# A hybrid attention layer on one core: loading the first gate's weight sums first, moving GLA's column products behind FoX's queries and keys, and making two of FF1's weight sums in DRAM

## The chip, the cores and the metric

The kernel runs on one core of a Trainium2 chip. The metric is the device time of one launch in microseconds (us); the median of three runs is given. A profile is taken of one further execution.

## What is computed

One layer of a streaming encoder for 512 frames of 1024 channels, all in float32. Three branches run side by side from the normalised input, are merged by gates, and a squared-ReLU MLP follows:

```python
u = rmsnorm(h, g_mix)
proj = u @ w_in          # GLA q,k,v,out-gate,alpha | FoX q,k,v,forget | memory q | 3 gates
o_gla = rmsnorm(gla_chunk_causal(gq * 64**-0.5, gk, gv, log_a), g_gla_head) * silu(gg)
o_fox = forgetting_attention(fq, fk, fv, log_sigmoid(ff + b_forget))   # 8 heads, causal
o_mem = memory_attention(mq, *split(rmsnorm(mem, g_mem) @ w_mem_kv))   # 256 tokens
gt = sigmoid(gates)
merged = gt[0] * (o_gla @ w_gla_o) + gt[1] * (o_fox @ w_fox_o) + gt[2] * (o_mem @ w_mem_o)
h = h + merged @ w_out
h = h + square(relu(rmsnorm(h, g_ffn) @ w_ff1)) @ w_ff2
return rmsnorm(h, g_final)
```

## The kernel before

Every product is made of three matmuls on halves that are split into a high part (a cast, on ScalarE, ACT) and a low part (the difference, on VectorE, DVE): high by high, high by low, low by high (`mm3`, L180 to L183). A weight tile is 128 x 1024; it is loaded by a DMA that SyncE (SP) issues (`load_w`, L164), cast (L171) and subtracted (L172), with three buffers of each kind in turn.

The larger products (GLA's values and output gate in `linear`, the three gates, FF1 and FF2) are Strassen-Winograd products: seven block products instead of eight, some of them of sums of weight blocks (named T for FF1 and the gates, G for `linear`) and of sums of u (named x or `xsum`, made by `u_sum` and split by `split`, L235). The sums of weights are made by DMAs that GpSimd (POOL) issues and that add to their destination (`accum_op`), in one of two ways:

- In DRAM, by `next_sum` (L134 to L146): behind each weight cast from the eighth on, POOL gets one DMA of a list, a copy (L143) or a sum (L141), that waits for that cast. The list before is `all_ops`: linear's G sums, then the T sums of FF1's first quarter. The later loads of G and T read these.
- In SBUF: a tile is loaded by SP and one or more sums are added to it. So it goes for the gates (`load_sum` L1207 and `plus` L1210, then the cast `high` L1223 and the low part `low` L1227), for FF1's quarters 1 to 3 (`sum_ring`, L1563 to L1578, with `tq`) and for FF2's factors (L1860).

The stages by time are: the front to 45 us; FoX's projections and softmax with products of other branches between them to 170; memory attention and the last of `linear` to 238; GLA to 298; the gates to 411; the merged output product to 480; FF1 and FF2 in four quarters to 817.

PE's order is written by hand, and a scheduler orders the others, but for sections under `in_order`, where ACT, DVE, SP (and in the gates POOL) keep the order of the code. The gates are such a section: the rounds begin with the raw loads that the first rounds want (`go(loads, 0)`), then the four T loads of the first gate, T1 and T2 for two halves each, then the sums into T1.

FoX's stage is a weave (L873): a list of steps on PE (scores, turns of the probabilities by matmuls with a unit matrix, L792 on, values) that draws units of other products between them, each with a share. Its filling list has, in order, FoX's pair 2 of queries and keys, the first sum of u, `linear(1)`, its split, pair 3, `linear(5)`, the second sum of u, `gla_k(0)`, `linear(2)`, the second split, `gla_q(0)` and `linear(6)`. `gla_k(0)` and `gla_q(0)` are column products of GLA's keys and queries. A softmax on DVE is custom operations on the scores (L781), reciprocals (L784) and a scaling of the probabilities `Pt` (L785), which the turns read. `u_sum` has three instructions for the first sum and two for the second, issued together behind a turn.

GLA begins with `decays(j)` (L1021): its matmuls read `la` (L1023), ACT makes `ex`, POOL sets one column of it (L1034), and DVE makes `kn` and three more of it, which PE turns (L1049).

Of the kernel before, what the change touches and what calls it, by code (L numbers as in the profile page):

```python
# [9 lines left out]
F32 = mybir.dt.float32  # L10
# [4 lines left out]
ALU = mybir.AluOpType  # L15
AX = mybir.AxisListType

P = 128
# [40 lines left out]
def hybrid_block(ctx, tc, chunks, wst, memT, xT, xN, gffn, gfin, wup, cst, out):  # L59
# [42 lines left out]

    tsum = {(n, i): dram.tile([1, P, 1024], F32, name=f"T{n}_{i}") for i in range(2) for n in (1, 2, 3, 4)}

    gsum = {n: dram.tile([2, P, 1024], F32, name=f"G{n}") for n in (1, 2, 3, 4)}

    def linear_ops():
        for n, src, add in ((1, "11", 0), (3, "12", 0), (1, "12", 1), (2, 1, 0), (2, "22", 1), (3, "22", 1), (4, 2, 0), (4, "21", 1)):  # L110
            if isinstance(src, str):
                i = index["N", "w_in", 4 * (src[0] == "2"), OFF["gv" if src[1] == "2" else "gg"]]
                src = wst[i:i + 2]
            else:
                src = gsum[src]
            yield gsum[n], src, add

    def sum_ops():
        for n, src, add in ((1, "11", 0), (3, "12", 0), (1, "12", 1), (3, "22", 1), (2, 1, 0), (2, "22", 1), (4, 2, 0), (4, "21", 1)):
            for i in range(2):  # L120
                k = index["F", 0, i, src] if isinstance(src, str) else None
                yield tsum[n, i], tsum[src, i] if k is None else wst[k:k + 1], add

    def all_ops():
        ff, lin = sum_ops(), linear_ops()
        for own in (3, 1, 1, 1, 1, 1):
            yield from islice(lin, own)
            yield from islice(ff, 1)
        yield from ff

    sums = all_ops()
    chunk_n, cast_now, low_now, hold = [0], [None], [None], [None]

    def next_sum(after):  # L134

        chunk_n[0] += 1
        if chunk_n[0] <= 7:
            return
        for to, src, add_ in islice(sums, 1):
            if add_:  # L140
                d = nc.gpsimd.dma_start(to, src, accum_op=ALU.add, max_dma_last_dim=8192)  # L141
            else:
                d = nc.gpsimd.dma_start(to, src)  # L143
            tc.add_manual_dep(d.ins, after.name, mybir.DependencyInfo(mybir.DependencyClass.Sync, mybir.DependencyReason.DATA),
                              reason="pace")

# [71 lines left out]
    def weave(steps, units, *gens, shares=None):  # L218

        fill = chain(*gens)  # L220
        done = 0
        shares = shares or [1] * len(steps)
        for i, st in enumerate(steps):
            st()
            due = units * sum(shares[:i + 1]) // sum(shares)
            while done < due and next(fill, fill) is not fill:
                done += 1
        run(fill)
# [306 lines left out]
    A11r, A12r, A21r, A22r = ([t[:, 4 * k:4 * k + 4, 256 * i:256 * i + 256] for t in (uhi, ulo)] for i in range(2) for k in range(2))  # L535
    A11, A12, A21, A22 = ([f(t) for t in a] for a in (A11r, A12r, A21r, A22r))

    def u_sum(n):

        x = xsum[n]  # L540
        if n == 1:
            nc.vector.tensor_tensor(x, A21[0], A22[0], op=ALU.subtract)
            nc.vector.tensor_tensor(x, x, A21[1], op=ALU.add)
            nc.vector.tensor_tensor(x, x, A22[1], op=ALU.subtract)
        else:
            nc.vector.tensor_tensor(x, xsum[1], A11[0], op=ALU.subtract)
            nc.vector.tensor_tensor(x, x, A11[1], op=ALU.subtract)

    def once(fn, *args):

        fn(*args)
        yield from ()
# [60 lines left out]
    with pool("fox") as xp:  # L613
# [211 lines left out]
        def gla_q(j):  # L825
            return proj(OFF["gq"] + P * j, lambda ps: nc.scalar.mul(gqT[j], ps, 0.125))

        def gla_k(j):
            return proj(OFF["gk"] + P * j, lambda ps: nc.scalar.copy(gkT[j], ps))
# [36 lines left out]
            early[n] = factor_tiles()  # L866
            split(*early[n], xsum[n])

        def early_sum(n):
            with tc.issue_after(live["turn"]):  # L870
                u_sum(n)

        weave([partial(fn, i) for fn, i, _ in steps], 80, fox_pair(2), once(early_sum, 1), linear(1, A11r), once(early_split, 1), fox_pair(3),  # L873
              linear(5, lambda: early[1]), once(early_sum, 2), gla_k(0), linear(2, A12r), once(early_split, 2), gla_q(0),
              linear(6, lambda: early[2]), shares=[n for *_, n in steps])


    mp = mst.enter_context(pool("merge", side="right"))
# [288 lines left out]
    with pool("outp") as op_:  # L1167
# [17 lines left out]
        def vec(to, x, y, op=ALU.add):  # L1185
            return nc.vector.tensor_tensor(to, x, y, op=op).ins
# [115 lines left out]
        def merge(g, i, c, half):  # L1302
            t = 2 * i + half
            x, a = th[g, i, c][:, half], half_of(acc[t], c)
            if g == 0:
                nc.vector.scalar_tensor_tensor(a, x, 1.0, a, op0=ALU.add, op1=ALU.mult)
            else:
                nc.vector.scalar_tensor_tensor(x, x, 1.0, half_of(ymem[t], c), op0=ALU.add, op1=ALU.mult)
                vec(a, a, x)

        def last_merge(c, t):
            x, a = th[2, t // 2, c][:, t % 2], half_of(acc[t], c)
# [53 lines left out]
        def go(when, i):  # L1366
            for fn, args in when.get(i, []):
                fn(*args)
# [3 lines left out]
        mh = ml = None  # L1372
        hN, now = [], [rounds[0]]
        with in_order(mybir.EngineType.Pool):
            go(loads, 0)
            loads[0] = []
            for other in range(2):
                for n in range(2):
                    load_sum(0, n, other)
            for n in range(2):  # L1380
                plus(0, n, 0, "12")
            for i, r in enumerate(rounds):
                now[0] = r
                if r == (2, 7):
                    omst.close()
                    mhp = late.enter_context(pool("mhl"))
                    mh, ml = (mhp.tile([P, KT, S], F32R, name=x) for x in ("mh", "ml"))
                if r == ("Y", 0):
                    hN += [h_tile(t, "h") for t in range(NT)]
                    gf = hp.tile([P, D], F32, tag="gf", name="gf")  # L1390
                    for t in (2, 3, 0, 1):
                        nc.sync.dma_start(hN[t], xN[t * P:(t + 1) * P, :])
                    nc.sync.dma_start(gf, gffn)
                if r == ("O", 0):
                    mst.close()
                    unp.append(late.enter_context(pool("un")))
                go(loads, i)
                go(early, i)
                n = NT if r[0] in ("Y", "O") else 2
                parts, due = todo[:1], [(r2, c) for r2 in rounds[i + 1:i + 2] for c in range(2)]  # L1400
                del todo[:1]
                for x in parts:
                    merge(*x)
                if i:
                    evac(rounds[i - 1], NT - 1 if rounds[i - 1][0] in ("Y", "O") else 1)
                for t in range(n):
                    mms(r, t)
                    if t == 0:
                        for x in due:
                            high(*x)  # L1410
                            low(*x)
                        bend()
                        go(after, i)
                    else:
                        evac(r, t - 1)
                    if r == ("Y", 0):
                        turn(t, 1)
                    if r == ("O", 1):
                        turn(t, 0)
            evac(r, n - 1)  # L1420
# [76 lines left out]
    with pool("ff") as yp:  # L1497
# [55 lines left out]
        def block(q, n, i):  # L1553
            if i > 1:
                return wst[index["B", q, i - 2, "21"]]
            if n in (1, 2, 3):
                return wst[index["F", q, i, {1: "11", 2: "21", 3: "22"}[n]]]
            n = {5: 1, 6: 2, 7: 3, 4: 4}[n]
            return tsum[n, i][0]

        tq = [yp.tile([P, 1024], F32, name=f"tq{i}") for i in range(2)]

        def sum_ring(q, n, i):  # L1563

            def plus(to, b):
                nc.gpsimd.dma_start(to, wst[index["F", q, i, b]], accum_op=ALU.add)

            if n == 7:
                raw = fetch(wst[index["F", q, i, "12"]])
                plus(raw, "22")  # L1570
                return split_b(raw)
            if n == 5:
                nc.sync.dma_start(tq[i], wst[index["F", q, i, "11"]])
                plus(tq[i], "12")
            w = split_b(tq[i])
            if n != 4:
                plus(tq[i], {5: "22", 6: "21"}[n])
            return w  # L1578

        def first_quarter():  # L1580
# [234 lines left out]

        def first_product(q, n):
            for i in range(2):
                w = sum_ring(q, n, i) if n in (5, 6, 7, 4) else ring(block(q, n, i))
                if n in (1, 5):
                    joint_product(n, w, (ev if n == 1 else od)[i][:, 1, :])  # L1820
                    continue
                ps = mmt([P, 2, 256])
                run(first_mms(n, w, ps))
                first_evac(n, i, ps)
# [365 lines left out]
```

## Time and profile before

| | |
|---|---|
| median of three runs | 820.36 us (819.77 to 821.3) |
| the profiled execution | 819.1 us |
| its span | 817.3 us |
| mean granted clock of PE | 0.988 |
| PE busy | 794.9 us, 97% |
| DVE busy | 621.5 us, 76% |
| ACT busy | 475.7 us, 58% |
| POOL busy | 100.1 us, 12% |
| PE's longest single wait | 5.7 us, for ACT's hi (L1223) |
| moved from DRAM | 156.25 MB, 214 GB/s over the span |

PE's share of the span is 97%. Its matmuls are pipelined, so a busy time can hold matmuls at half speed: the granted clock in a window tells. The view of waits lists how long PE stood, for which engine and line. The DMA share is the mean busy share of the 16 DMA engines of the core.

### The profile page before, as it was taken

The numbers are of one execution on the slowest core, as the hardware profiler recorded it, in microseconds if no ns is written. First come the engines' busy times: TensorE is split into PE (matmuls) and PEld (weight loads), VectorE is DVE, ScalarE is ACT, GpSimd is POOL, SyncE is SP. The second block draws the span as 40 slices with busy tenths as digits, with TensorE's granted clock in tenths as the row PEclk, the third lists the DMA queues.
The fourth block names the chain that finished last, engine by engine and source line by source line (L and its number), as shares of the span: only waits on it lengthen the run. The fifth ranks groups of instructions, "written<-read, shape, count | busy, mean of one in ns | idle before, by whom it ended". The sixth has DMA issues, their size and how long they took to land.

```text
span 817.3 us, 11675 instructions
## 1 busy us (share of the span) xinstructions
PE 794.9 (97%) x4351; PEld 677.8 (83%) x4351; DVE 621.5 (76%) x971; ACT 475.7 (58%) x746; POOL 100.1 (12%) x137
## 2 busy tenths in 40 slices
PE   9999989999999987999999999999999999999995
PEld 7888868888888875888888889977997899889974
DVE  6878989755876757667776558788789778987896
ACT  7756666634564345556434446864676367646854
POOL 0001001110200212020200001012110211111011
PEclk9999999999999997999999999999999999999998
DMA  9355768892832259988926318998999998998653
GB/s 355 135 164 165 234 237 217 264 267 78 254 108 83 73 178 189 250 191 248 204 80 242 121 50 237 296 229 214 224 247 215 220 235 231 216 251 226 156 90 116
DMA packets 42249, 159.15 MB, mean 195 GB/s; under 512 B 4944, under 2 KB 5648, under 8 KB 40976
## 3 DMA queue, kind: packets, MB, share of 16 engines
q0 software_dynamic: 13120, 58.73, 36.3%
q1 hardware_dynamic: 27712, 95.72, 32.2%
q10 hardware_dynamic: 1360, 3.96, 1.5%
q8 instruction: 34, 0.56, 0.3%
q14 instruction: 23, 0.19, 0.1%
HBM read 156.25 MB, written 18.91 MB: 214 GB/s over the span
## 4 chain that ended last, share of the span: by engine, by line
PE 78%; DVE 8%; DMA 8%; issue 3%; ACT 2%; POOL 0%; SPq 0%; POOLq 0%; DVEq 0%; ACTq 0%
PE mm L181 15%; PE mm L182 15%; PE mm L183 14%; PE mm L1462 10%; DMA b<-in_wst_dram 4%; PE a L182 4%; PE a L183 4%; PE a L181 4%; PE mm L1810 3%; DMA wb<-in_wst_dram 2%; PE mm L412 1%; PE mm L1811 1%; PE a L425 1%; DVE wlo L172 1%; DVE lo L1598 1%
## 5 line engine op out<-in xcount | busy, mean ns | idle before, releaser
L172 DVE TENSOR_TENSOR wlo<-raw,whi 128x1024 fp32r<-128x1024 f32 x44 | 53.8, 1224 | 30.6 <-ACT whi L171 29.8
L171 ACT CAST whi<-raw 128x1024 fp32r<-128x1024 f32 x44 | 46.3, 1053 | 49.2 <-PE mm L182 14.9
L1462 PE MATMUL mm<-u,hi 128*128 128x256 f32 x384 | 64.7, 283 | 0.0
L1462 PEld LDWEIGHTS mm<-u,hi 128*128 128x128 f32 x384 | 56.4, 189 | 0.1
L182 PE MATMUL mm<-lo,ch 128*128 128x512 f32 (+1 forms) x132 | 51.4, 389 | 0.9 <-DVE lo L1522 0.9
L183 PE MATMUL mm<-hi,cl 128*128 128x512 f32 (+1 forms) x132 | 51.0, 386 | 0.0
L181 PE MATMUL mm<-hi,ch 128*128 128x512 f32 (+1 forms) x132 | 51.0, 386 | 0.0
L1521 ACT CAST hi<-raw 128x1024 fp32r<-128x1024 f32 x34 | 35.8, 1053 | 25.8 <-PE mm L1462 12.2
L1522 DVE TENSOR_TENSOR lo<-raw,hi 128x1024 fp32r<-128x1024 f32 x34 | 41.6, 1223 | 10.3 <-ACT hi L1521 10.3
L1462 PE MATMUL mm<-u,lo 128*128 128x256 f32 x192 | 47.5, 283 | 0.0
L1462 PE MATMUL mm<-u2s,hi 128*128 128x256 f32 x288 | 47.3, 283 | 0.0
L1521 ACT CAST hi<-b 128x1024 fp32r<-128x1024 f32 x26 | 27.3, 1050 | 31.5 <-PE mm L183 19.4
L181 PE MATMUL mm<-uhl,whi 128*128 128x512 f32 x112 | 44.6, 398 | 0.0
L1860 POOL DMA_DIRECT2D b<-in_wst_dram x30 | 25.9, 874 | 146.3 <-DMA b<-in_wst_dram 43.8
L1227 DVE TENSOR_TENSOR lo<-wb,hi 128x1024 fp32r<-128x1024 f32 x21 | 25.3, 1223 | 24.2 <-ACT hi L1223 24.2
L183 PE MATMUL mm<-uhl,wlo 128*128 128x512 f32 x112 | 43.7, 390 | 0.0
L182 PE MATMUL mm<-uhl,whi 128*128 128x512 f32 x112 | 43.7, 390 | 0.0
L1462 PEld LDWEIGHTS mm<-u2s,hi 128*128 128x128 f32 x288 | 41.6, 190 | 0.0
L1522 DVE TENSOR_TENSOR lo<-b,hi 128x1024 fp32r<-128x1024 f32 x26 | 31.5, 1223 | 9.2 <-ACT hi L1521 9.2
L182 PE MATMUL a<-lo,ch 128*128 128x512 f32 (+1 forms) x96 | 37.3, 389 | 1.1 <-DVE lo L1598 0.7
L181 PE MATMUL a<-hi,ch 128*128 128x512 f32 (+1 forms) x96 | 37.2, 387 | 0.4 <-DVE h L1515 0.4
L183 PE MATMUL a<-hi,cl 128*128 128x512 f32 (+1 forms) x96 | 37.0, 386 | 0.0
(535 smaller groups left out, 2398.4 us busy)
## 6 DMA issues: line engine op xcount, KB each, us to landing
raw<-in_wst_dram SPq DMA_DIRECT2D x114, 512.0 KB
b<-in_wst_dram POOLq DMA_DIRECT2D x32, 512.0 KB, 6.7
wb<-in_wst_dram POOLq DMA_DIRECT2D x24, 512.0 KB, 7.9
tq<-in_wst_dram POOLq DMA_DIRECT2D x18, 512.0 KB, 9.6
b<-in_wst_dram SPq DMA_DIRECT2D x16, 512.0 KB
T<-in_wst_dram POOLq DMA_DIRECT2D x12, 512.0 KB, 5.8
wb<-in_wst_dram SPq DMA_DIRECT2D x12, 512.0 KB
G<-in_wst_dram POOLq DMA_DIRECT2D x4, 1024.0 KB, 9.1
```

The source lines that it names most:

```text
L171: cast = nc.scalar.copy(hi, raw)
L172: low_now[0] = nc.vector.tensor_tensor(lo, raw, f(hi), op=ALU.subtract).ins
L181: nc.tensor.matmul(ps, lh, rh, start=start, stop=False, skip_group_check=on)
L182: nc.tensor.matmul(ps, lh, rl, start=False, stop=False, skip_group_check=on)
L183: nc.tensor.matmul(ps, ll, rh, start=False, stop=stop, skip_group_check=on)
L412: nc.tensor.matmul(kps[h], w[:, h * P:(h + 1) * P], x[:, k, :], start=k == p == 0, stop=k == KT - 1 and p == 2)
L1227: nc.vector.tensor_tensor(lo, source(r, c), f(hi), op=ALU.subtract)
L1462: nc.tensor.matmul(ps[:, a, :], x[:, a, k, :], y[:, s, k, :], start=start, stop=stop, skip_group_check=go is not None)
L1521: split_now[0] = nc.scalar.copy(hi, raw).ins
L1522: split_now[1] = nc.vector.tensor_tensor(lo, raw, f(hi), op=ALU.subtract).ins
L1810: nc.tensor.matmul(ps, wh[:, a, k, :], u[:, k], start=k == 0, stop=False, skip_group_check=True)
L1860: nc.gpsimd.dma_start(to[i], wst[index["B", q, i, x]], accum_op=ALU.add)
```

## The change

It has three parts.

**First gate.** The loads of T1 and the sums into it stand before the raw loads, and T2's loads behind them. On SP, in the place where the gates begin (`wb` are the T tiles, `raw` weights as they are), before:

```order
L164 DMA raw_2964<-in_wst_dram 128x1024
L164 DMA raw_2998<-in_wst_dram 128x1024
L164 DMA raw_3026<-in_wst_dram 128x1024
L164 DMA raw_3028<-in_wst_dram 128x1024
L164 DMA raw_3030<-in_wst_dram 128x1024
L1207 DMA wb_3022<-in_wst_dram 128x1024
L1207 DMA wb_3023<-in_wst_dram 128x1024
L1207 DMA wb_3024<-in_wst_dram 128x1024
L1207 DMA wb_3025<-in_wst_dram 128x1024
```

and on SP at the same place after the change:

```order
L169 DMA raw_2976<-in_wst_dram 128x1024
L169 DMA raw_3010<-in_wst_dram 128x1024
L1208 DMA wb_3034<-in_wst_dram 128x1024
L1208 DMA wb_3035<-in_wst_dram 128x1024
L169 DMA raw_3042<-in_wst_dram 128x1024
L169 DMA raw_3044<-in_wst_dram 128x1024
L169 DMA raw_3046<-in_wst_dram 128x1024
L1208 DMA wb_3036<-in_wst_dram 128x1024
L1208 DMA wb_3037<-in_wst_dram 128x1024
```

T1's two loads moved ahead of three raw loads, and T2's two stay behind them.

**FoX's weave.** `gla_k(0)` comes right behind FoX's pair 2, where `linear(1)` was begun, and the rest follows it in the order of the diff; the sums of u are issued one instruction at a time. On DVE, the end of the second of the four softmaxes (`ri` reciprocals, `Pt` probabilities, `s` the split of the first sum of u, `oT` the values of the step before, `wlo` a weight's low part), before:

```order
L785 TENSOR_SCALAR Pt_1091<-Pt_1091,ri_1057 128x128
L235 TENSOR_TENSOR s_1277<-x_470,s_1276 128x1024
L785 TENSOR_SCALAR Pt_1096<-Pt_1096,ri_1057 128x256
L785 TENSOR_SCALAR Pt_1111<-Pt_1111,ri_1060 128x128
L785 TENSOR_SCALAR Pt_1116<-Pt_1116,ri_1060 128x256
L785 TENSOR_SCALAR Pt_1101<-Pt_1101,ri_1057 128x384
L785 TENSOR_SCALAR Pt_1121<-Pt_1121,ri_1060 128x384
L784 RECIPROCAL ri_1057<-rs_1056 128x1
L784 RECIPROCAL ri_1060<-rs_1059 128x1
L818 TENSOR_TENSOR oT_1006<-a_1147,th_1156 64x512
L172 TENSOR_TENSOR wlo_1283<-raw_1280,whi_1282 128x1024
L785 TENSOR_SCALAR Pt_1106<-Pt_1106,ri_1057 128x512
```

and on DVE at the end of the same softmax after the change:

```order
L785 TENSOR_SCALAR Pt_1122<-Pt_1122,ri_1066 128x256
L784 RECIPROCAL ri_1066<-rs_1065 128x1
L784 RECIPROCAL ri_1063<-rs_1062 128x1
L785 TENSOR_SCALAR Pt_1107<-Pt_1107,ri_1063 128x384
L785 TENSOR_SCALAR Pt_1127<-Pt_1127,ri_1066 128x384
L784 RECIPROCAL ri_1066<-rs_1065 128x1
L785 TENSOR_SCALAR Pt_1112<-Pt_1112,ri_1063 128x512
L785 TENSOR_SCALAR Pt_1132<-Pt_1132,ri_1066 128x512
L818 TENSOR_TENSOR oT_1012<-a_1153,th_1162 64x512
L240 TENSOR_TENSOR ofl_121<-oT_1012,ofh_117 128x512
L177 TENSOR_TENSOR wlo_1398<-raw_1395,whi_1397 128x1024
```

The split and the wlo no longer stand among the scalings of `Pt`; nor does a sum of u stand in the part of this softmax ahead of these rows.

**T1 and T3 of FF1.** For quarters 1 to 3 these are made in DRAM, as for quarter 0, but in DMAs of two tiles (1 MB) each: T3's three copies and three sums behind the other sums, in GLA; T1's behind the round (2,7), the last of the gates, in the product with w_out (O). `sum_ring` then loads T1 into `tq` and T3 as a whole, and keeps the sums for T2 and T4; twelve DMAs that add in SBUF are gone. The list for `linear` and quarter 0 is also in another order. On POOL, from the last sum of quarter 0 on (`at` and `ex` belong to GLA), before:

```order
L141 DMA T_0_80<-in_wst_dram 64x2048
L141 DMA T_1_84<-in_wst_dram 64x2048
L1076 MEMSET at_2599 128x512
L1076 MEMSET at_2600 128x512
L1034 MEMSET ex_2514 128x8
L1034 MEMSET ex_2659 128x8
```

and on POOL from the same place after the change:

```order
L146 DMA T_4_90<-in_wst_dram 64x2048
L148 DMA T_1_82<-in_wst_dram 16x16384
L148 DMA T_2_84<-in_wst_dram 16x16384
L148 DMA T_3_86<-in_wst_dram 16x16384
L146 DMA T_1_82<-in_wst_dram 128x2048
L1077 MEMSET at_2608 128x512
L1077 MEMSET at_2609 128x512
L1035 MEMSET ex_2521 128x8
L146 DMA T_2_84<-in_wst_dram 128x2048
L146 DMA T_3_86<-in_wst_dram 128x2048
L1035 MEMSET ex_2669 128x8
```

Three copies and one sum stand ahead of the first `ex`, and two sums between it and the second.

The core of the diff:

```diff
-    def all_ops():
-        ff, lin = sum_ops(), linear_ops()
-        for own in (3, 1, 1, 1, 1, 1):
+    def first_ops():
+        lin = linear_ops()
+        ff = sum_ops(((1, "11", 0), (3, "12", 0), (1, "12", 1), (3, "22", 1), (2, 1, 0), (2, "22", 1), (4, 2, 0), (4, "21", 1)), (0, 4))
+        for own, others in ((4, 1), (1, 3), (1, 1), (1, 1), (1, 0)):
             yield from islice(lin, own)
-            yield from islice(ff, 1)
+            yield from islice(ff, others)
         yield from ff
-
-    sums = all_ops()
+        yield from sum_ops(((3, "12", 0), (3, "22", 1)), (1, 2, 3))
+
+    sums = [first_ops(), sum_ops(((1, "11", 0), (1, "12", 1)), (1, 2, 3))]
+    late_on, merged = [], [None]
...
-        weave([partial(fn, i) for fn, i, _ in steps], 80, fox_pair(2), once(early_sum, 1), linear(1, A11r), once(early_split, 1), fox_pair(3),
-              linear(5, lambda: early[1]), once(early_sum, 2), gla_k(0), linear(2, A12r), once(early_split, 2), gla_q(0),
-              linear(6, lambda: early[2]), shares=[n for *_, n in steps])
+        weave([partial(fn, i) for fn, i, _ in steps], 80, fox_pair(2), gla_k(0), once(early_sum, 1, 0), fox_pair(3), once(early_sum, 1, 1),
+              linear(1, A11r), once(early_sum, 1, 2), once(early_split, 1), gla_q(0), once(early_sum, 2, 0), linear(5, lambda: early[1]),
+              once(early_sum, 2, 1), once(early_split, 2), linear(2, A12r), linear(6, lambda: early[2]),
+              shares=[n for *_, n in steps])
...
         with in_order(mybir.EngineType.Pool):
+            for n in range(2):
+                load_sum(0, n, 0)
+                plus(0, n, 0, "12")
             go(loads, 0)
             loads[0] = []
-            for other in range(2):
-                for n in range(2):
-                    load_sum(0, n, other)
             for n in range(2):
-                plus(0, n, 0, "12")
+                load_sum(0, n, 1)
...
+                        if r == (2, 7):
+                            late_on.append(1)
...
-            if n == 7:
-                raw = fetch(wst[index["F", q, i, "12"]])
-                plus(raw, "22")
-                return split_b(raw)
             if n == 5:
-                nc.sync.dma_start(tq[i], wst[index["F", q, i, "11"]])
-                plus(tq[i], "12")
+                nc.sync.dma_start(tq[i], tsum[1, q][i])
             w = split_b(tq[i])
             if n != 4:
-                plus(tq[i], {5: "22", 6: "21"}[n])
+                nc.gpsimd.dma_start(tq[i], wst[index["F", q, i, {5: "22", 6: "21"}[n]]], accum_op=ALU.add)
             return w
```

More of the change, by code (lines that the diff above doesn't have):

```diff
@@ L101, in small @@
         return pool_.tile([P, LINE], F32, tag=tag, name=name or nm(tag), bufs=bufs)[:, :n]
-    tsum = {(n, i): dram.tile([1, P, 1024], F32, name=f"T{n}_{i}") for i in range(2) for n in (1, 2, 3, 4)}
+    tsum = {(n, q): dram.tile([2 if 0 < q < 4 else 1, P, 1024], F32, name=f"T{n}_{q}") for q in range(5) for n in (1, 2, 3, 4)
+            if n in (1, 3) or not 0 < q < 4}
     gsum = {n: dram.tile([2, P, 1024], F32, name=f"G{n}") for n in (1, 2, 3, 4)}
@@ L116, in linear_ops, with sum_ops @@
             yield gsum[n], src, add
[L118 to L122, printed above, removed]
-    def all_ops():
-        ff, lin = sum_ops(), linear_ops()
-        for own in (3, 1, 1, 1, 1, 1):
+    def sum_ops(ops, qs):
+        for n, src, add in ops:
+            for q in qs:
+                i = index["F", q % 4, 0 if q else 1, src] if isinstance(src, str) else None
+                yield tsum[n, q], tsum[src, q] if i is None else wst[i:i + (2 if 0 < q < 4 else 1)], add
+    def first_ops():
+        lin = linear_ops()
+        ff = sum_ops(((1, "11", 0), (3, "12", 0), (1, "12", 1), (3, "22", 1), (2, 1, 0), (2, "22", 1), (4, 2, 0), (4, "21", 1)), (0, 4))
+        for own, others in ((4, 1), (1, 3), (1, 1), (1, 1), (1, 0)):
             yield from islice(lin, own)
-            yield from islice(ff, 1)
+            yield from islice(ff, others)
         yield from ff
-    sums = all_ops()
+        yield from sum_ops(((3, "12", 0), (3, "22", 1)), (1, 2, 3))
+    sums = [first_ops(), sum_ops(((1, "11", 0), (1, "12", 1)), (1, 2, 3))]
+    late_on, merged = [], [None]
     chunk_n, cast_now, low_now, hold = [0], [None], [None], [None]
@@ L138, in next_sum @@
             return
[L139 to L143, printed above, removed]
+        for to, src, add_ in islice(sums[len(late_on)], 1):
+            with tc.issue_after(merged[0]) if late_on else ExitStack():
+                if add_:
+                    d = nc.gpsimd.dma_start(to, src, accum_op=ALU.add, max_dma_last_dim=8192)
+                else:
+                    d = nc.gpsimd.dma_start(to, src)
             tc.add_manual_dep(d.ins, after.name, mybir.DependencyInfo(mybir.DependencyClass.Sync, mybir.DependencyReason.DATA),
@@ L536, in hybrid_block, with u_sum @@
     A11, A12, A21, A22 = ([f(t) for t in a] for a in (A11r, A12r, A21r, A22r))
[L538 to L547, printed above, removed]
+    def u_sum(n, step):
+        x, y, op = {1: ((A21[0], A22[0], ALU.subtract), (xsum[1], A21[1], ALU.add), (xsum[1], A22[1], ALU.subtract)),
+                    2: ((xsum[1], A11[0], ALU.subtract), (xsum[2], A11[1], ALU.subtract))}[n][step]
+        nc.vector.tensor_tensor(xsum[n], x, y, op=op)
     def once(fn, *args):
@@ L867, in early_split, with early_sum @@
             split(*early[n], xsum[n])
-        def early_sum(n):
+        def early_sum(*args):
             with tc.issue_after(live["turn"]):
-                u_sum(n)
-        weave([partial(fn, i) for fn, i, _ in steps], 80, fox_pair(2), once(early_sum, 1), linear(1, A11r), once(early_split, 1), fox_pair(3),
-              linear(5, lambda: early[1]), once(early_sum, 2), gla_k(0), linear(2, A12r), once(early_split, 2), gla_q(0),
-              linear(6, lambda: early[2]), shares=[n for *_, n in steps])
+                u_sum(*args)
+        weave([partial(fn, i) for fn, i, _ in steps], 80, fox_pair(2), gla_k(0), once(early_sum, 1, 0), fox_pair(3), once(early_sum, 1, 1),
+              linear(1, A11r), once(early_sum, 1, 2), once(early_split, 1), gla_q(0), once(early_sum, 2, 0), linear(5, lambda: early[1]),
+              once(early_sum, 2, 1), once(early_split, 2), linear(2, A12r), linear(6, lambda: early[2]),
+              shares=[n for *_, n in steps])
     mp = mst.enter_context(pool("merge", side="right"))
@@ L1308, in merge @@
                 nc.vector.scalar_tensor_tensor(x, x, 1.0, half_of(ymem[t], c), op0=ALU.add, op1=ALU.mult)
-                vec(a, a, x)
+                merged[0] = vec(a, a, x)
         def last_merge(c, t):
@@ L1558, in block @@
             n = {5: 1, 6: 2, 7: 3, 4: 4}[n]
-            return tsum[n, i][0]
+            return tsum[n, q][i] if q else tsum[n, 0 if i else 4][0]
         tq = [yp.tile([P, 1024], F32, name=f"tq{i}") for i in range(2)]
         def sum_ring(q, n, i):
-            def plus(to, b):
-                nc.gpsimd.dma_start(to, wst[index["F", q, i, b]], accum_op=ALU.add)
-            if n == 7:
-                raw = fetch(wst[index["F", q, i, "12"]])
-                plus(raw, "22")
-                return split_b(raw)
             if n == 5:
-                nc.sync.dma_start(tq[i], wst[index["F", q, i, "11"]])
-                plus(tq[i], "12")
+                nc.sync.dma_start(tq[i], tsum[1, q][i])
             w = split_b(tq[i])
             if n != 4:
-                plus(tq[i], {5: "22", 6: "21"}[n])
+                nc.gpsimd.dma_start(tq[i], wst[index["F", q, i, {5: "22", 6: "21"}[n]]], accum_op=ALU.add)
             return w
@@ L1817, in first_product @@
             for i in range(2):
-                w = sum_ring(q, n, i) if n in (5, 6, 7, 4) else ring(block(q, n, i))
+                w = sum_ring(q, n, i) if n in (5, 6, 4) else ring(block(q, n, i))
                 if n in (1, 5):
```

## The prediction

> **What bounds the kernel now.** I read the page first, then PE's waits, then windows around the longest of them, then the timelines of the engines inside those windows. The page's first part names the bound:
>
> ```profile
> PE 794.9 (97%) x4351; PEld 677.8 (83%) x4351; DVE 621.5 (76%) x971; ACT 475.7 (58%) x746; POOL 100.1 (12%) x137
> ```
>
> TensorE (PE) is busy for 794.9 us of the span of 817.3 us. No part of the change removes a matmul, so only two things can move the end: the 22.4 us in which PE isn't busy, and busy time that is long because the clock is low. The view of PE's waits sorts the first of these (waited for; us in total, times, longest):
>
> ```profile
> PE mm L181 <- ACT hi L1223: 5.7, 1, 5.7
> PE a L792 <- DVE Pt L785: 3.0, 2, 2.5
> ...
> PE mm L182 <- DVE lo L1522: 0.9, 2, 0.5
> PE mm L182 <- DVE lo L1227: 0.9, 2, 0.5
> PE a L182 <- DVE lo L1598: 0.7, 1, 0.7
> PE a L181 <- DVE h L1515: 0.4, 1, 0.4
> ```
>
> Two places hold most of it: the first gate (5.7 and the 0.9 of L1227) and one turn of FoX's probabilities (3.0). The lines L1515, L1522 and L1598 are FF1 and FF2. Windows cut at the clock's steps show the second loss (length; busy PE, PEld, DVE, ACT, POOL; granted clock; DMA share; GB/s):
>
> ```profile
> 105.30:108.70 3.40, 3.03 (x10) 2.22 (x10) 2.99 (x7) 1.45 (x3) 0.00 (x0) 0.50 0.74 231
> ...
> 306.70:310.10 3.40, 0.04 (x1) 0.05 (x1) 0.07 (x1) 1.04 (x1) 0.00 (x0) 0.50 1.07 249
> ...
> 313.50:316.90 3.40, 3.00 (x7) 1.99 (x7) 3.40 (x5) 2.81 (x4) 2.02 (x3) 0.50 0.93 153
> ```
>
> Behind each of the two stalls the granted clock is 0.50: for one such window in FoX, and from 306.7 to 316.9 at the gate. So a stall costs its wait and then matmuls at half speed. The whole price of each stall is read from PE's own rows, by when the first matmul at full speed starts and when it would have started.
>
> **Part A, the first gate's T1.** PE's timeline there (start, length; the bracket is idle time before and its releaser):
>
> ```profile
> 303.72 0.39 PE L182 MATMUL a<-f0l,uhl 128*128 128x512 f32 x1
> 303.95 0.39 PE L183 MATMUL a<-f0h,uhl 128*128 128x512 f32 x1
> 310.06 0.80 PE L181 MATMUL mm<-hi,s 128*128 128x512 f32 x1 [5.72 <-ACT hi L1223]
> ...
> 316.93 0.39 PE L181 MATMUL mm<-hi,s 128*128 128x512 f32 x1
> ```
>
> At full speed a matmul starts 0.23 us after the one before it. Twelve matmuls start from 310.06 on, and the thirteenth, at 316.93, is the first at full speed. Unstalled, the first would start at 303.95 + 0.23 = 304.18 and the thirteenth at 304.18 + 12 x 0.227 = 306.90. The stall's whole price is 316.93 - 306.90 = 10.0 us.
>
> What PE waits for is T1 of the first gate, weights that are loaded (L1207), added to by a DMA (L1210) and only then cast (L1223). The chain of waits shows the way there:
>
> ```profile
> 294.84 0.42 SPq L1207
> ...
> 295.31 6.23 DMA wb<-in_wst_dram
> ...
> 301.82 10.38 DMA wb<-in_wst_dram
> ```
>
> The loads go out from 294.84, because SP stands in a raw load until DVE's last wlo, and the four of them share the DMA engines for 6.2 us; the second sum is out at 301.82 and lands 10.4 us later, at 312.2. After the change SP issues T1's two loads ahead of those raw loads. Their tiles lie where `la` was, so they still wait for the last matmul that reads it, and the two sums stand on POOL behind the four stat operations:
>
> ```profile
> 254.90 1.05 PE L1023 MATMUL a<-cst_s,la 128*128 128x128 f32 x8
> ```
>
> ```profile
> 286.00 1.01 POOL L1106 TENSOR_TENSOR stat<-stat,mhalf 128x4 f32<-128x4 f32 x1 [1.32 <-DVE stat L1105]
> ```
>
> The first condition is met at 256, and the loads need a few microseconds, with a DMA share that is low there. The second is met at 287.0, and that is what ends last. For how long a sum takes I have the page's DMA rows (KB each, median us from issue to landing):
>
> ```profile
> wb<-in_wst_dram POOLq DMA_DIRECT2D x24, 512.0 KB, 7.9
> tq<-in_wst_dram POOLq DMA_DIRECT2D x18, 512.0 KB, 9.6
> ...
> G<-in_wst_dram POOLq DMA_DIRECT2D x4, 1024.0 KB, 9.1
> ```
>
> A sum issued at 287.0 and one 0.9 us later land at 294.9 and 295.8 by the 7.9, at 298.3 by the 10.4 of the chain. ACT needs 1.05 us a tile for hi and DVE 1.2 us for lo, so the first tile is ready at 297 to 300.6, ahead of 304.18. The wait goes, with 3 us of slack or more; what is late next is T2, whose loads now stand behind the raw loads as T1's did, but which the next rounds ask for, 5.5 us a round later. Term: -10.0 us. Bounds: -10.0, and -5 should 1 or 2 us of wait remain with one half-clock window.
>
> Here the Trainium skill speaks of size ("TensorE: Matmul & The Clock Gate", "What's actually happening"): half clock comes after an idle window of 3.4 us, and full clock after one busy window. By that the half clock would have lasted one window behind 310.06, about 8 matmuls 0.2 us late, and the term would be 8.2 us; the trace disagrees, since the window from 313.50 has PE busy for 3.00 of 3.40 and the clock is still 0.50, and I keep the 10.0 of the rows.
>
> **Part B, FoX's weave.** The stalled turn, and the like one a step later:
>
> ```profile
> 101.93 0.39 PE L792 MATMUL a<-cst_s,Pt 128*128 128x128 f32 x2
> 102.78 0.33 PE L792 MATMUL a<-cst_s,Pt 128*128 128x128 f32 x1 [0.46 <-DVE Pt L785]
> 105.62 0.47 PE L792 MATMUL a<-cst_s,Pt 128*128 128x128 f32 x1 [2.51 <-DVE Pt L785]
> ...
> 108.73 0.50 PE L181 MATMUL mm<-whi,uhl 128*128 128x512 f32 x1
> 109.07 0.39 PE L182 MATMUL mm<-wlo,uhl 128*128 128x512 f32 x1
> ```
>
> ```profile
> 126.47 0.60 PE L792 MATMUL a<-cst_s,Pt 128*128 128x128 f32 x4
> ...
> 127.48 0.47 PE L181 MATMUL mm<-uhl,whi 128*128 128x512 f32 x1
> ```
>
> The later turn goes through in 1.01 us. Four matmuls, the last at 108.73, stand between the stalled turn and the first one at full speed, at 109.07. Unstalled, that one would start at 101.93 + 1.01 + 4 x 0.227 = 103.85, so the stall's price is 5.2 us. DVE's timeline tells why the probabilities were late:
>
> ```profile
> 97.53 1.22 DVE L544 TENSOR_TENSOR x<-x,uhl 128x1024 f32<-128x1024 f32 x1
> ...
> 100.45 1.22 DVE L235 TENSOR_TENSOR s<-x,s 128x1024 fp32r<-128x1024 f32 x1
> ...
> 103.94 1.23 DVE L172 TENSOR_TENSOR wlo<-raw,whi 128x1024 fp32r<-128x1024 f32 x1
> ```
>
> Three foreign operations stand among the softmax's own (a sum of u, its split, a wlo), 1.22 + 1.22 + 1.23 = 3.7 us, and two more sums of u stand right ahead of it. After the change none of the five stands there: the sums of u are single instructions issued steps apart, the split comes several units later, and the wlo stands behind the last Pt. What released the last wait came at 105.62; without the three it comes at 101.95, and earlier still as the softmax can begin sooner. PE asks for it at 105.62 - 2.51 = 103.11 now and at about 102.7 without the wait of 0.46, so 0.7 us of slack at the least. Term: -5.2 us. Bounds: -5.2, and 0 if evictions and splits of the column product that is moved to this place fill the same gap. The guests don't vanish: by the order, the next softmax gets one sum of u and the one after it one more than before, 1.2 us. No wait of PE stands at either now; I cost that at nothing, and at up to 1.2 us if that cover is gone.
>
> **Part C, T1 and T3 of FF1 made in DRAM.** In quarters 1 to 3 twelve accumulating DMAs (tq's first and all of T3's) leave POOL's queue, and each moved 512 KB beside loads that the products wait for; twelve DMAs of 1 MB come in GLA and in the rounds behind the last gate, where PE's waits above show nothing. What this can give back is bounded by FF's waits in the list: 0.9 + 0.7 + 0.4 = 2.0 us; none of these is a wait for T1 or T3 itself, they wait for FF2's factors, behind the same queue. Bounds: 0 and -2.0; I take -1.2, nearer to the second, because tq's 9.6 us against 7.9 for the gates' sums shows how full that queue is. The load of tq now waits for a sum in DRAM that was finished tens of microseconds earlier.
>
> **Sum.** 817.3 - 10.0 - 5.2 - 1.2 = 800.9 us of span. The profiled execution took 819.1, 1.8 over its span, so 802.7; the median of the three runs, 820.36, is 1.3 above the profiled one, so the forecast for the median is 804.0 us. About 0.2% (1.6 us) is what a measurement of this kernel can tell from no change.
>
> **The rivals.**
>
> First, FoX's stall stays: DVE's order is new there, and gla_k(0)'s product brings its own evictions. For it: 0.7 us of slack is little. Against it: by the order no guest is left ahead of the last Pt, and the earlier start isn't counted in that slack. Then 804.0 + 5.2 = 809.2 us. Chance 0.10.
>
> Second, a wait moves into the stretch behind FoX, where the DMA engines are full. The first row is a window (DMA share 1.04), the next are DVE's and PE's timelines, the last the DMA rows for 130 to 170:
>
> ```profile
> 160.00:170.00 10.00, 10.00 (x53) 8.56 (x52) 7.08 (x11) 6.19 (x9) 2.11 (x3) 1.00 1.04 265
> ```
>
> ```profile
> 181.52 1.22 DVE L172 TENSOR_TENSOR wlo<-raw,whi 128x1024 fp32r<-128x1024 f32 x1
> ```
>
> ```profile
> 184.63 0.39 PE L183 MATMUL mm<-uhl,wlo 128*128 128x512 f32 x1
> ```
>
> ```profile
> T<-in_wst_dram POOLq DMA_DIRECT2D x6, 512.0 KB, 7.4
> ...
> G<-in_wst_dram POOLq DMA_DIRECT2D x2, 1024.0 KB, 10.6
> ```
>
> The wlo is ready at 182.74, and PE uses it at 184.63: 1.9 us of slack. The change swaps a T copy and a G sum on POOL, so that the larger one falls into the full stretch, 10.6 - 7.4 = 3.2 us more. If all of it reaches that load, PE waits 1.3 us, and 3.0 with one half-clock window (3.4 us at half speed loses 1.7). Half-way, 804.0 + 2.2 = 806.2 us. Against it: the load may have been early. Chance 0.20.
>
> Third, part A doesn't do what it says: the sums are held on POOL past 300 by something queued ahead (the ex and at memsets, the stat operations, all waiting for GLA), and the gate's stall remains: 804.0 + 10.0 = 814.0 us. Against it, the stat rows end at 287.0 without any sum in their way. Chance 0.07.
>
> Fourth, slower. T3's sums now stand on POOL among GLA's memsets: the sum for quarter 1, which waits for its own copy, stands ahead of the memset of ex, and kn, on DVE, waits for that memset, with qpos, kp, qneg and the next wlo queued behind kn.
>
> ```profile
> 229.56 1.05 ACT L171 CAST whi<-raw 128x1024 fp32r<-128x1024 f32 x1
> ```
>
> ```profile
> 241.89 0.11 POOL L1034 MEMSET ex<- 128x8 f32 x1 [17.51 <-ACT ex L1032]
> ```
>
> ```profile
> 246.76 0.49 PE L1049 MATMUL a<-cst_s,kn 128*128 128x128 f32 x3
> ```
>
> The copy goes out at 230.6, behind the cast that paces it; PE asks for kn at 246.76, so the memset may come until about 245.9, and the copy may take 15.3 us. The page's row for 1 MB says 9.1. The mechanism costs time only past 15.3 us, and it makes the kernel slower only past 15.3 + 16.4 = 31.7 us (the 16.4 of the other terms); at 35 us the time is 804.0 + 19.7 = 823.7, more with half clock behind the wait. Chance 0.05, of which 0.01 ends within 0.2% of the old time.
>
> A page of the Trainium skill speaks for it ("DMA: Bandwidth & Descriptors", "Queues, rings and completion order"): each DMA engine takes turns between queues, packet by packet. By that the copy, beside a steady stream of loads, would take twice its 9.1 us, 18.2, and kn would be 2.9 us late. In this trace the DMA share of that stretch is too low for a steady stream, and the price stays out of the sum.
>
> **How the numbers follow.** The forecast has the remaining chance, 0.58, and its own range is 802.5 to 806 (part C at its bounds, the runs' spread). The range of 8 in 10 takes in the second rival and the first (0.88 in all), 801.5 to 810.0; it leaves out the third and the fourth. All but the fourth are faster by over 1.6 us: 0.95 faster, 0.01 within, 0.04 slower.
>
> **What would show it.** Right: no wait of PE on hi L1223 (now L1224) and none above 0.5 us on Pt, no clock below 1.00 from 90 to 330, T1's two loads on SP and its sums on POOL at about 282 (5 us earlier than the stat rows now), a list of waits that holds FF alone. Wrong: a new PE wait between 140 and 185 on wlo (second rival), or on kn in GLA (fourth), a half-clock window at either, or waits in FF that have grown, which would mean that T1 and T3 in DRAM didn't free the queue.

## The result, and the profile after

| | before | after |
|---|---|---|
| median | 820.83 us (819.77 to 821.45, 4 runs) | 812.97 us (811.54 to 813.27, 4 runs) |
| profiled execution, span | 819.1, 817.3 us | 813.05, 811.3 us |

The ratio is 0.9902, with a 95% interval from 0.9885 to 0.9919: the change is faster by 7.9 us. The forecast was 804.0 us, range 801.5 to 810.0; the direction is right, and the time lies 3 us above the range. The two profiled executions differ by less, 6.0 us of span, since the one before was 1.7 us faster than the median of its kernel; the stages below are read from these two.

First the page's busy line and PE's waits of the changed kernel:

```profile
PE 793.0 (98%) x4351; PEld 678.6 (84%) x4351; DVE 620.3 (76%) x971; ACT 474.2 (58%) x746; POOL 97.4 (12%) x137
```

```profile
PE a L186 <- ACT mh L1322: 2.6, 1, 2.6
PE a L186 <- ACT qh L239: 1.9, 1, 1.9
...
PE mm L186 <- ACT hi L1224: 1.0, 1, 1.0
PE a L188 <- DVE ql L240: 1.0, 1, 1.0
...
PE a L186 <- DVE h L1518: 0.4, 1, 0.4
PE mm L187 <- DVE lo L1525: 0.4, 1, 0.4
```

The 5.7 and the 3.0 are gone, and FF's waits have shrunk from 2.0 to 0.8. But two waits head the list that weren't in it: on `mh` in O, the product with w_out (2.6), and on `qh` and `ql` in memory attention (1.9 and 1.0). Windows over the places tell both halves of the story (the columns are those of the prediction's windows):

```profile
100.00:120.00 20.00, 20.00 (x118) 16.78 (x117) 18.29 (x52) 13.12 (x31) 0.99 (x2) 1.00 0.72 247
...
300.00:320.00 20.00, 20.00 (x90) 16.57 (x89) 17.24 (x17) 12.62 (x15) 5.23 (x6) 1.00 0.96 217
```

```profile
170.00:180.00 10.00, 7.13 (x32) 5.75 (x31) 5.31 (x7) 2.69 (x4) 0.52 (x1) 0.91 1.06 292
...
420.00:430.00 10.00, 10.00 (x52) 8.26 (x51) 1.67 (x2) 2.87 (x5) 1.00 (x2) 1.00 1.02 251
430.00:440.00 10.00, 10.00 (x52) 8.23 (x51) 8.34 (x13) 1.59 (x4) 0.62 (x1) 1.00 1.02 272
440.00:450.00 10.00, 7.25 (x32) 5.30 (x31) 3.76 (x5) 3.56 (x5) 0.00 (x0) 0.89 0.77 302
```

FoX and the first gate are whole now, at clock 1.00. From 170 and from 440 PE is busy for 7 of 10 us and the clock falls, and the DMA share there, or just ahead, is over 1.

PE does 4351 matmuls in both kernels, and behind FoX in the same order, so each matmul's start can be set against its twin's in the other trace. A negative shift means that the changed kernel is ahead. By stage it changes so:

| place | forecast | measured | shift so far |
|---|---|---|---|
| front | 0 | -0.6 | -0.6 |
| FoX's turn | -5.2 | -5.1 | -5.7 |
| memory attention | 0 | +5.3 | -0.4 |
| first gate | -10.0 | -10.1 | -10.4 |
| a later round of that gate | 0 | +1.0 | -9.4 |
| O | 0 | +6.2 | -3.2 |
| FF | -1.2 | -2.6 | -5.8 |

**Memory attention.** PE's timeline there:

```profile
174.54 0.39 PE L188 MATMUL mm<-uhl,wlo 128*128 128x512 f32 x1
176.81 0.39 PE L186 MATMUL a<-mkh,qh 128*128 128x256 f32 x1 [1.88 <-ACT qh L239]
...
178.31 0.58 PE L188 MATMUL a<-mkh,ql 128*128 128x256 f32 x1 [0.99 <-DVE ql L240]
...
181.72 0.39 PE L186 MATMUL mm<-whi,ofh 128*128 128x512 f32 x1
```

`qh` is a cast of PE's own result and needs no weight. ACT's timeline shows why it was late:

```profile
175.22 1.04 ACT L176 CAST whi<-raw 128x1024 fp32r<-128x1024 f32 x1 [1.74 <-DMA raw<-in_wst_dram]
176.18 0.58 ACT L239 CAST qh<-mm 128x512 fp32r<-128x512 f32 x1
```

The cast of a weight that PE reads only behind these matmuls stands ahead of it on ACT and waits for its load; on DVE `ql` stands behind that weight's wlo in the same way. The chain of waits leads back through two loads that took 14.2 and 11.0 us:

```profile
147.58 14.17 DMA raw<-in_wst_dram
...
164.17 10.98 DMA raw<-in_wst_dram
...
177.56 0.70 DVE ql L240
```

In the kernel before the same two were ready long ahead of PE (rows of ACT, DVE and PE):

```profile
175.49 0.57 ACT L234 CAST qh<-mm 128x512 fp32r<-128x512 f32 x1
```

```profile
176.88 0.69 DVE L235 TENSOR_TENSOR ql<-mm,qh 128x512 fp32r<-128x512 f32 x1
```

```profile
180.00 0.28 PE L181 MATMUL a<-mkh,qh 128*128 128x256 f32 x1
```

There `qh` had 3.9 us of slack (ready at 176.06, read at 180.00) and `ql` 2.7 (177.57 and 180.23). In the changed kernel they are ready at 176.76 and 178.25, 0.7 us later than before, and PE is done with what stands ahead of them 5.2 us sooner.

**O.** PE, and then the longest step of the chain:

```profile
444.78 0.60 PE L1320 MATMUL mm<-cst_s,acc 128*128 128x128 f32 x4
447.99 0.80 PE L186 MATMUL a<-hi,mh 128*128 128x512 f32 x1 [2.61 <-ACT mh L1322]
...
454.62 0.39 PE L188 MATMUL a<-hi,ml 128*128 128x512 f32 x1
```

```profile
422.63 23.68 DMA raw<-in_wst_dram
```

A load of 512 KB took 23.7 us. On SP it is the second of the eight loads in the last row here:

```profile
417.33 2.18 SPq L1393 DMA_DIRECT2D h<-in_xN_dram  x4
419.55 0.53 SPq L1394 DMA_DIRECT2D gf<-in_gffn_dram  x1
420.18 35.44 SPq L169 DMA_DIRECT2D raw<-in_wst_dram  x8
```

Five loads of `h` and `gf`, 2.5 MB, go out ahead of it, and beside them T1's three sums; the `mh` that PE asks for stands on ACT behind the cast of that weight. The same 20 us of PE's work in the kernel before, without the sums, come 9.4 us later:

```profile
429.40:439.40 10.00, 10.00 (x52) 8.26 (x51) 6.23 (x8) 4.12 (x6) 0.00 (x0) 1.00 1.01 400
439.40:449.40 10.00, 10.00 (x51) 8.23 (x50) 7.15 (x10) 3.97 (x7) 0.00 (x0) 1.00 0.25 80
```

### The profile page after: what moved, and what is told of

It is laid out like the page before. It is cut to its first block, busy times and chain, and to the rows that moved or that the text cites. A ratio compares the mean times of both kernels' runs of the same rounds, so it can differ in the third digit from the quotient of the medians.

```text
span 811.3 us, 11675 instructions
## 1 busy us (share of the span) xinstructions
PE 793.0 (98%) x4351; PEld 678.6 (84%) x4351; DVE 620.3 (76%) x971; ACT 474.2 (58%) x746; POOL 97.4 (12%) x137
## 4 chain that ended last, share of the span: by engine, by line
PE 84%; DMA 8%; DVE 5%; issue 1%; ACT 1%; SPq 0%; POOLq 0%; DVEq 0%; POOL 0%; ACTq 0%
PE mm L1465 16%; PE mm L186 14%; PE mm L187 14%; PE mm L188 14%; DMA raw<-in_wst_dram 6%; PE a L188 4%; PE a L186 4%; PE a L187 4%; PE mm L1805 3%; PE mm L1806 1%; DMA xt<-in_xT_dram 1%; PE mm L715 1%; DVE wlo L177 1%; PE a L430 1%; DMA mem_s<-in_memT_dram 1%
```

## The experiments

The kernels share their runs of the kernel before, whose median in each batch is given beside the ratio.

**Part A alone.** The loops of the first gate as in the diff, in the kernel before.

> The kernel before with part A alone (T1 of the first gate loaded and summed ahead of the raw loads). By the comparison of the two traces the gate's stall was worth 10.1 us, and a wait of 1.0 us two rounds later came with it: 820.8 - 10.1 + 1.0 = 811.7 us, no half-clock window from 300 to 320. Rival: the gate's stall needs the other parts too (an emptier queue); then it stays near 820 us.

Measured: 810.69 us against 820.1, ratio 0.9886 (0.9858 to 0.9914). The gate's stall gives 10.1 us in the trace, a later round takes 0.6. FF is 0.9 us shorter, without part C. Part A stands by itself, and alone it is as fast as the whole change: the intervals overlap.

**Part B alone.** The weave and the single sums of u, with the DRAM sums in their old order.

> The kernel before with part B alone (FoX's weave and the sums of u), the list of DRAM sums as before. FoX's stall goes, 5.1 us. Theory one, that the wait behind FoX (on qh and ql) comes from the new order of the DRAM sums, which put the sum of G3 beside two others: no wait there, 815.7 us. Theory two, that PE now comes 5 us too early into a stretch where the DMA engines are full: the same wait as in the changed kernel, price 4.9 us, 820.6 us.

Measured: 821.18 us against 820.1, ratio 1.0006 (0.9985 to 1.0027). PE's waits (of this kernel, with its line numbers):

```profile
PE mm L181 <- ACT hi L1219: 7.0, 2, 5.9
PE a L181 <- ACT qh L234: 1.7, 1, 1.7
...
PE a L183 <- DVE ql L235: 1.0, 1, 1.0
```

FoX's wait is gone and the new one stands there, with the old order of the sums. So theory one falls: the new order isn't needed for the wait. By the twins PE is 4.8 us ahead of the kernel before at 160 and 1.1 us behind it at 190: what FoX gave is taken back by the stretch behind it, into which PE now comes 5 us sooner; 4.9 us of it go at this wait, 1.0 at one on `s` ahead of it.

**Part C alone.**

> The kernel before with part C alone: the new order of the DRAM sums, T1 and T3 of FF1 in DRAM. FoX's and the gate's stalls stay. FF gives 2.6 us, O takes 6.3 us by its wait on mh (the loads for O late behind T1's sums): 820.8 - 2.6 + 6.3 = 824.5 us. Theory one would add a wait behind FoX of up to 4.9 us (829); theory two has none there, since PE doesn't come earlier. Rival for O: its wait needs the gates to be faster; then 818 us.

Measured: 824.86 us against 820.1, ratio 1.0052 (1.0021 to 1.0084): slower, by 0.5%. Its waits, beside those of FoX and the gate that it keeps:

```profile
PE a L186 <- ACT mh L1326: 2.4, 1, 2.4
PE mm L187 <- DVE wlo L177: 1.5, 1, 1.5
```

O's wait comes without the faster gates, so it is part C's own. That the time came out near 824.5 is luck in part: by the twins O took 4.6 us and not 6.3, FF gave 1.2 and not 2.6, and GLA and the gates took 1.6 and 1.3 us that nobody had counted. No wait stands behind FoX, as theory two has it. The 1.5 on wlo is new: it stands in GLA, where T3's sums go out, and I return to it.

**G3's sum earlier.** One line of the list, in the changed kernel:

```diff
-        for own, others in ((4, 1), (1, 3), (1, 1), (1, 1), (1, 0)):
+        for own, others in ((4, 1), (1, 1), (1, 2), (1, 1), (1, 0)):
```

> The changed kernel with one change of the list: the sum of G3 stands ahead of two copies of T3 instead of behind them, so that the stretch from 141 to 165 holds what it held in the kernel before. Theory one: the waits on qh and ql go with their half clock, 813.0 - 4.9 = 808.1 us. Theory two: they stay, 813.0 us.

Measured: 810.86 us against 820.1, ratio 0.9895 (0.9847 to 0.9943). The runs spread over 8.8 us, so the median says little, the trace more: the wait on `qh` is gone and the one on `ql` stays, at full clock, and from 160 to 190 PE is 3.7 us faster than in the changed kernel.

```profile
PE a L186 <- ACT mh L1322: 2.4, 1, 2.4
...
PE a L188 <- DVE ql L240: 1.0, 1, 1.0
```

Theory two as I put it falls too: the order of the sums does act. Together with part B alone, what is left is that both count: PE earlier, and bytes that the sums move just ahead.

**Linear's sums first.**

```diff
-        for own, others in ((4, 1), (1, 3), (1, 1), (1, 1), (1, 0)):
+        for own, others in ((8, 0),):
```

> The changed kernel with the whole list of linear's G sums ahead of FF1's T sums, so that from 141 to 163 us POOL issues four copies of 512 KB where it issued a sum and a copy of 1 MB and a sum of 512 KB. If the wait behind FoX is a matter of how many bytes the sums move there, it goes with ql's 1.0 too: 813.0 - 4.9 = 808.1 us. If PE simply comes too early whatever the sums are, 811 us or more, as with G3's sum moved by one or two places. A rival mishap: the G sums now press on FoX's loads from 100 to 140, a new wait there.

Measured: 806.61 us against 819.68, ratio 0.9847 (0.9823 to 0.9872). Both waits behind FoX are gone, and no new one has come for them:

```profile
160.00:170.00 10.00, 10.00 (x48) 8.42 (x47) 6.15 (x8) 3.85 (x5) 1.55 (x2) 1.00 1.03 248
170.00:180.00 10.00, 10.00 (x52) 8.50 (x51) 6.18 (x10) 4.13 (x9) 1.03 (x2) 1.00 0.79 266
```

The stretch is shorter by the whole 5.3 us (0.5 and 4.8 by the twins). The larger sums went out earlier. In the changed kernel the DMA share was 0.62, 0.84 and 0.42 in the windows of 10 us from 110 to 140 and 1.02 from 150 to 160; here it is 0.71, 1.05, 0.76 and 0.90. A full share alone makes no wait: PE stands nowhere from 120 to 130, with 1.05.

**O's raw loads ahead of h.** In the round before the last product, `go(loads, i)` now comes ahead of the loads of `h` and `gf`:

```diff
                 if r == ("Y", 0):
                     hN += [h_tile(t, "h") for t in range(NT)]
                     gf = hp.tile([P, D], F32, tag="gf", name="gf")
-                    for t in (2, 3, 0, 1):
-                        nc.sync.dma_start(hN[t], xN[t * P:(t + 1) * P, :])
-                    nc.sync.dma_start(gf, gffn)
...
                 go(loads, i)
+                if r == ("Y", 0):
+                    for t in (2, 3, 0, 1):
+                        nc.sync.dma_start(hN[t], xN[t * P:(t + 1) * P, :])
+                    nc.sync.dma_start(gf, gffn)
```

> The changed kernel with the two raw loads for the last round of O issued ahead of the five loads of h and gf on SP, instead of behind them. Theory one: O's wait on mh is a load that stands on SP's queue behind 2.5 MB, while T1's sums take half of the DMA engines; with the order turned the load comes some 10 us sooner, the wait goes: 813.0 - 6.2 = 806.8 us. Theory two: the sums alone make it late; a wait of 1 us or more stays, above 810 us.

Measured: 809.16 us against 819.68, ratio 0.9878 (0.9847 to 0.991). The wait on `mh` is gone and O is 5.8 us shorter; the median fell by less, 3.8 us, since memory attention took 1.0 us more in the profiled execution and the runs spread over 4 us. What was late was a load behind others that nobody needed yet.

**Without T1's sums.**

```diff
-    sums = [first_ops(), sum_ops(((1, "11", 0), (1, "12", 1)), (1, 2, 3))]
+    sums = [first_ops(), iter(())]
...
-                nc.sync.dma_start(tq[i], tsum[1, q][i])
+                nc.sync.dma_start(tq[i], wst[index["F", q, i, "11"]])
```

> The changed kernel without the six DMAs that make T1 for quarters 1 to 3 in DRAM; tq is loaded from one block alone, so FF1's products with T1 and what is added to it are of other weights. If T1's DMAs are what makes O's loads late, the wait on mh goes: 813.0 - 6.2 = 806.8 us. If h's loads or the faster gates do it, the wait stays and the time is 813 us.

Measured: 808.29 us against 819.68, ratio 0.987 (0.985 to 0.989). No wait on `mh`, O shorter by 6.25 us. So T1's DMAs (copies and sums weren't tried apart) and the place on SP are both needed for the wait: taking either away takes it all away.

**Both orders turned.**

> Both orders at once: linear's sums first, and O's raw loads ahead of h. If both waits go and nothing new comes, 813.0 - 4.9 - 6.2 = 801.9 us, near the blind forecast of 804.0; if either stays, 807 to 808 us.

Measured: 802.36 us against 819.68, ratio 0.9799 (0.9777 to 0.9822). All that is left of PE's waits over 0.5 us:

```profile
PE a L328 <- DVE warm L325: 1.2, 1, 1.2
PE mm L186 <- ACT hi L1224: 0.8, 1, 0.8
PE a L188 <- DVE ml L1323: 0.8, 1, 0.8
```

This beats both kernels; against the forecast of 804.0 it is what the change would have been without the two new waits.

**What part C is worth.** Parts A and B with linear's sums first, T1 and T3 in SBUF as before, and the kernel with both orders once more beside it.

> Parts A and B with linear's sums first, and T1 and T3 of FF1 made in SBUF as in the kernel before (no part C). No wait behind FoX and none in O without T1's sums there. If part C is worth the 2.6 us that FF shows between the two traces: 802.4 + 2.6 = 805.0 us. If FF's waits come and go by themselves (FF alone was 0.9 us shorter with part A alone, 2.3 us longer with part B alone, neither with part C), then part C is worth nothing that shows: 801 to 803 us.

> The kernel with both orders turned, beside the one without part C on the same chip: 802.4 us as measured at first, so that the difference of the two is part C's worth, 2.6 us or nothing.

Measured: 804.45 us without part C, ratio 0.9792 (0.9761 to 0.9823), and 803.4 with it, 0.9774 (0.9741 to 0.9807), both against 821.26. The difference of 1.0 us lies within both intervals, so the medians don't show what part C is worth. Without part C FF has these waits:

```profile
PE mm L180 <- DVE lo L1516: 1.4, 3, 0.5
PE a L180 <- DVE lo L1516: 1.2, 2, 0.8
```

By the twins its FF is 3.5 to 4.8 us longer than in the two executions with part C, and its O 0.9 to 1.2 us shorter. With part C, the second execution has in GLA the wait that part C alone had:

```profile
258.22 0.50 PE L187 MATMUL mm<-wlo,om 128*128 128x512 f32 x1 [1.56 <-DVE wlo L177]
```

The first execution of the same kernel has none there, and it keeps most of FF's gain (4.1 us less span than without part C); in the second the gain and the costs nearly cancel (1.0 us less). With part C alone, the chain of waits leads from that wlo, over what DVE does in its order, back to a load that went out beside T3's copies and first sum and took 15.3 us:

```profile
237.12 15.26 DMA raw<-in_wst_dram
```

So T3's DMAs leave the loads of GLA little slack, and the wait comes in some executions and not in others. No experiment moved these loads or T3's DMAs by themselves.

## Why the prediction was wrong

Two steps failed: part B's gain was carried through the full stretch behind FoX, where the slack was smaller than the gain (+5.3 us), and T1's DMAs were costed at nothing in O (+6.2). In the span the forecast was 800.9 us and the profiled execution took 811.3, 10.4 more; the medians hide 1.4 us of that, by luck, because the 1.3 that the text put between the profiled execution and the median wasn't there after the change.

**The gate (right).** -10.0 forecast, -10.1 measured, and -10.1 with part A alone. The reasoning by the condition that ends last holds: the sums stood behind POOL's stat operations and were out right behind them, in time.

```profile
285.64 1.01 POOL L1107 TENSOR_TENSOR stat<-stat,mhalf 128x4 f32<-128x4 f32 x1 [1.31 <-DVE stat L1106]
286.60 1.82 POOL L1211 DMA_DIRECT2D wb<-in_wst_dram  x2
```

The text had them at about 282, 5 us earlier; those 5 us had been lost in memory attention. What the text named as late next, T2, wasn't: its sums landed at 315.15 and 317.96, and PE reads it from 320.14 on without a wait. In the round behind, PE stood 1.0 us; shortly before, ACT had stood in the cast of a tile for which the third sum into T1 landed late, at 323.64:

```profile
323.72 1.05 ACT L1224 CAST hi<-wb 128x1024 fp32r<-128x1024 f32 x1 [1.84 <-DMA wb<-in_wst_dram]
```

That round loses 1.0 us with part B alone and 1.5 with part C alone, where the first gate is as before, so this isn't part A's own.

**FoX (right as a price, wrong as a gain).** -5.2 forecast, -5.1 measured at that place. But the gain was counted as if all behind it would just move up by 5 us. Part B alone shows that it doesn't: 821.18 against 820.1, a difference within its interval.

**The second rival (right in place, not in cause).** The text put a wait into this stretch with a chance of 0.20 and 0 to 3.0 us; it measured 5.3. The step that failed is the slack. The text took it from one wlo and its first use, 1.9 us, at the time when PE came there in the kernel before, and didn't take off the 5.2 us by which part B brings PE forward. It also looked at the wrong instructions: the wait fell on `qh` and `ql`, which stand behind the cast and wlo of the weight before that one and use neither weight, on engines that keep their order. Their slack was 3.9 and 2.7 us, less than 5.2. The rival's own cause, a larger sum in place of a copy, was to make a load 3.2 us later; `qh` and `ql` were ready 0.7 us later than before, and part B alone has the wait with the old order. That moving the sums takes the wait away (3.7 us for G3's, all of it for linear's first) shows that the loads, not PE's arrival alone, set it. Which of the DMAs that were out at 144, 147 and 151 made a load take 14 us wasn't tried one by one.

**Part C (the term that was wrong).** The text says that the twelve DMAs of 1 MB come "in GLA and in the rounds behind the last gate, where PE's waits above show nothing", and costs them at nothing. That PE doesn't wait says nothing of how near the loads are to being late. In the kernel before, the DMA share was 1.01 from 429.4 to 439.4 already, with SP's row of `h`, `gf` and raw loads, and 0.25 in the 10 us behind; the sums made 20 full microseconds of it, and O took 6.2 us. Had this term been in the sum, it would have read 810.2, just past the range's edge. FF's -2.6 went past the bound of -2.0; part of FF's waits come and go without part C (-0.9 with part A alone, and 2.3 us more than before with part B alone), so the bounds of 0 and -2.0, from one trace's list of waits, were too narrow.

**The rivals that didn't come.** FoX's stall didn't stay, part A did what it says, and no wait stood at `kn`: the fourth rival's memset of `ex` wasn't late. T3's DMAs in GLA did go with a cost, in two executions, but on a raw weight's wlo, 1.5 and 1.6 us.

## What to carry to other kernels

When a stall goes, all that comes behind it comes sooner, and loads that were on time by less than that become the next stall; so price the next place where the DMA engines are full before counting the gain. A transfer that is moved costs nothing only where the DMA share has room and where no urgent load stands behind others on its queue: look at the share and at the queue, not at the waits of the engine that doesn't wait yet. On an engine that keeps its order, a cast that waits for its load holds up whatever stands behind it, also work that never needed that load.

## What the hardware showed besides

The half clock behind a stall isn't tied to the stall's length alone. Memory attention's wait is nearly the same in the changed kernel (1.88 and 0.99 us) and in the kernel without T1's sums (1.75 and 0.99), but behind it the clock is 0.50 in the first and 1.00 in the second. The traces show when the clock changes: in the changed kernel at 178.12, 181.53, 447.77, 454.60 and 806.17 us, all whole multiples of 3.413 us apart. Windows cut there, from the changed kernel:

```profile
174.71:178.12 3.41, 0.73 (x3) 0.30 (x2) 1.79 (x2) 1.53 (x2) 0.52 (x1) 1.00 1.03 264
178.12:181.53 3.41, 3.23 (x13) 3.03 (x14) 0.82 (x2) 0.94 (x1) 0.00 (x0) 0.50 0.98 370
```

and from the kernel without T1's sums, counted back by 3.413 us from its change at 800.88:

```profile
172.83:176.24 3.41, 2.11 (x10) 1.41 (x8) 0.22 (x2) 1.14 (x2) 0.00 (x0) 1.00 1.07 258
176.24:179.65 3.41, 1.97 (x13) 1.76 (x14) 2.55 (x3) 0.40 (x1) 0.52 (x1) 1.00 1.07 339
```

In the first nearly the whole wait falls into one window, which leaves PE 0.73 us of work, and the next is at half clock; in the second it is split, with 2.11 and 1.97 us, and the clock stays. The stretch took 1.4 us less there. The Trainium skill ("TensorE: Matmul & The Clock Gate", "What's actually happening") says that the activity window runs free of the kernel; by that the same wait can fall into one window or be split between two, and these two traces agree.

A full DMA engine isn't one rate: the share is 1.01 at 400 GB/s with plain loads (429.4 to 439.4 before) and 1.02 at 251 and 272 GB/s with T1's sums among them (420 to 440 after). By queue in those 20 us after (packets, MB, share of the 16 engines; the first is POOL's, the second SP's):

```profile
q0 software_dynamic: 405, 3.01, 72.9%
q1 hardware_dynamic: 596, 2.20, 28.7%
```

A megabyte of the sums took 1.9 times as much of the engines' time as a megabyte of the loads.
